# Retention's products as products of f16 halves, in a two-layer hybrid encoder trunk

## The chip, the core and the metric

One core of one Trainium2 chip runs the whole program. The metric is the device time of one execution in microseconds (us). All tables and lines below are from one profiled execution, unless they are said to be a median of runs. The engines are called PE (TensorE, the matrix engine; PEld is its loading of weights), DVE (VectorE), ACT (ScalarE), POOL (GpSimd) and SP (SyncE, which here only issues DMAs). L123 is line 123 of the kernel before, unless the kernel after is named.

## The reference

```python
D_MODEL, SEQ, DEPTH, CHUNK = 1024, 2048, 2, 64      # f32 throughout
...
def chunkwise_retention(q, k, v, cos, sin):
    q = apply_rotary(q, cos, sin)
    k = apply_rotary(k, cos, sin) * (dk ** -0.5)
    log_g = jnp.log1p(-jnp.exp2(-5.0 - jnp.arange(h)))
    intra_decay = jnp.exp(jnp.abs(idx[:, None] - idx[None, :])[None] * log_g[:, None, None])
    k_decay = jnp.exp((CHUNK - 1 - idx)[None, :] * log_g[:, None])
    q_decay = jnp.exp((idx + 1.0)[None, :] * log_g[:, None])
    chunk_decay = jnp.exp(CHUNK * log_g)
...
    att = jnp.einsum("bnihd,bnjhd->bnhij", qc, kc) * intra_decay[None, None]
    o_intra = jnp.einsum("bnhij,bnjhe->bnihe", att, vc)
    kv = jnp.einsum("bnjhd,hj,bnjhe->bnhde", kc, k_decay, vc)
    def step(state, kv_n):
        return state * chunk_decay[None, :, None, None] + kv_n, state
    _, states = lax.scan(step, zeros, moveaxis(kv, 1, 0))
    o_inter = jnp.einsum("bnihd,hi,bnhde->bnihe", qc, q_decay, states)
    return rms_norm(o_intra + o_inter)

def hybrid_layer(x, norm_gain, w_in, w_out, rel_bias, cos, sin):
    hn = rms_norm(x, norm_gain)
    proj = hn @ w_in                              # (2048, 1024) @ (1024, 4096)
    aq, ak, av, ag, rq, rk, rv, rg = jnp.split(proj, cuts, axis=-1)       # 512 columns each
    ya = chunked_rel_attention(aq, ak, av, rel_bias)       # 8 heads x 64, own chunk + 8 before
    yr = chunkwise_retention(rq, rk, rv, cos, sin)         # 4 heads x 128
    y = jnp.concatenate([ya * silu(ag), yr * silu(rg)], axis=-1)
    return x + y @ w_out
```

Two such layers follow one another, and the result is normalised once more. The change concerns retention (the four einsums above and the rotation in front of them) and the scale of the norm's gain.

## The kernel before

**Halves.** All dense products of the kernel are exact to about f32 although PE is fed with f16: each operand is split into a high half (the f16 rounding) and a low half (what is left, again in f16), and a product is three f16 products that add up in one PSUM bank: high times high, high times low, low times high. The splitting takes a copy on ACT (the high half) and a subtraction on DVE (the low half), in every place. So that nothing overflows or vanishes in f16, weights and rows are scaled by powers of two found from their sums of squares (`norm_scale`, L141); the inverse scales are undone later by column factors (`mul_cols`, L178, used in `T_units`, L341, and `V_units`, L397). Retention alone computes with f32 operands.

**Stages.** A startup (L1131 to L1228, an order written out by hand as a string of step names) loads x, normalises the first eight tiles of 128 tokens and prepares the first weights. Then each layer `l` runs four groups `s`. A group is two attention heads and one retention head. Each group runs four blocks `n` of 512 tokens. For a block, `dense_T` (L605) computes the four projections that are needed transposed, q, k, rq and rk (j = 0 to 3), each as 24 matmuls of 512 columns (L688), and `dense_V` (L695) computes the value and gate projections of the four tiles `a` of the block, 24 matmuls of 512 columns each (L708). These are cut into rounds: after every 8 matmuls the generator yields, so a block has 24 rounds. After the groups of a layer follows the output projection `wout` (L966), in the same rounds.

**What runs between the rounds.** `run` (L1043) does three things after each round: `tick`, which issues what `later(k, fn)` has put off by k rounds; one step of `attention` (L727) of the previous block, which itself steps `retention` (L802); and some steps of the background work in `bg` (conversion of the next weights `prep_T`, `prep_V`, `prep_O`, the rotary tables, the norms of later input tiles). The order of PE, ACT, DVE and POOL is the order in which the program issues: `manual_schedule` (L40) fixes it, and each of these engines executes in order. SP's queue is fixed by hand in the startup only; later the scheduler places its DMAs.

**Attention.** A block has 8 units (4 tiles by 2 heads), one per three rounds. A unit's scores go to one PSUM tile S, of which there is one buffer (L742, matmuls L749 and L750); DVE adds the bias and finds the maximum (L753), ACT takes the exponential (L756) and a high half (L758), POOL the low half (L759), a transposing DMA turns both (L761, tile pT), and one unit later PE multiplies with v (L769 to L771).

**Rotation.** ACT moves the projection of rq or rk out of PSUM into `rot` (L639, f32, 128x512), SP copies it with its halves exchanged to `swp` (L643, L644), three rounds later POOL multiplies both with the tables of cosines and sines and adds them (L647 to L649, the function `turn`).

**Retention.** Each tile of 128 tokens has two steps, in different rounds. In the first, PE computes the scores of keys and queries (L809) and turns the keys with a product by the identity (L812), ACT copies the turned keys with the key decay as a column factor (L814, ktok), and DVE multiplies the scores with the decay mask (L815, dT). In the second, PE adds dT times rv (L818) and the queries times the state (L820) in one place and ktok times rv, the tile's part of the state, in another (L822); DVE updates the state (L825); ACT squares the output for its norm (L831), DVE (L832) and POOL (L833) make the factor of the norm. Two rounds later DVE applies factor and gate (L837).

**Memory.** PSUM has three pools: psD, 2 banks for the dense products, psS for the scores, psR with 4 banks for retention, attention's output and small things. In SBUF, `w4` has four buffers of 128x1024 f32 for weights on their way in and tiles of x; `wh` and `wl` hold the converted weights; `hT` holds the normalised, transposed input of a layer, 128x8x512 per block and half.

**Scale of the gain.** `gain_scale` (L160) squares the norm's gain, sums it over the partitions by a product with ones (`allsum`, L319), and takes an inverse power of two from the exponent; it is called once in the startup, ahead of the first token's norm (`rms_of`, L195), and once in group 1 for layer 2, its two steps put off by 2 and 10 rounds (L1255 to L1257).

## Time and profile before

| | before |
|---|---|
| median of 3 runs | 2116.52 us (2115.85 to 2116.53) |
| profiled execution, whole time | 2114.12 us |
| its span, first to last instruction | 2112.3 us |
| mean clock that TensorE was granted | 0.994 of full |
| instructions | 37,845, of them 13,636 matmuls |
| DMA | 305 MB, 63% of 16 engines' time |

The retention lines on PE, by the trace: 128 products L809, 120 transposes L812, 128 products L818, 120 L820 and 120 L822 (an f32 product counts as two matmuls in the records). DMA issues that the change touches or that lie beside what it touches (the row of the page: tiles, queue, count, KB each, median us from issue to landing):

```profile
q<-qq SPq DMA_DIRECT2D x128, 128.0 KB, 2.6
swp<-rot SPq DMA_DIRECT2D x128, 128.0 KB, 2.4
```

To read the lines of a timeline: start in us from the span's start, length in us, engine, line, operation, output<-inputs by the names of tiles, shapes; in square brackets how long the engine had been idle and what released it. A matmul's shown length is modelled: what it costs PE is the distance from its start to the next one's. A line of the stretches gives, for a window of time, its length and then the busy time and the instructions of PE, PEld, DVE, ACT and POOL, the granted clock as a share, the DMA engines' busy share and the GB/s moved. For orientation: startup to about 50 us, the first group to about 230, then the groups of layer 1 to about 890, its output projection to about 1100, layer 2 after that.

### The profile page before, as it was taken

How to read it: one execution, taken by the hardware profiler on the slowest of the kernel's cores; microseconds unless marked ns; L12 is line 12 of the kernel's file. 1: busy time of each engine (PE TensorE's matmuls, PEld its weight loads, DVE VectorE, ACT ScalarE, POOL GpSimd, SP SyncE). 2: the span in 40 equal slices, each digit the busy share in tenths (PEclk: the TensorE clock that was granted, in tenths of full speed). 3: DMA queues.
4: the chain of work that ended last, by engine and by line, in shares of the span. 5: the costliest groups of instructions: out<-in, count | busy, mean ns of one | idle time of the engine just before them, and what ended most of it. 6: DMA issues, size and time to landing. Idle time of an engine off the chain costs nothing. (4 is left out here: it accounts for less than half of the span.)

```text
span 2112.3 us, 37845 instructions
## 1 busy us (share of the span) xinstructions
PE 2039.2 (97%) x13636; PEld 1109.4 (53%) x13636; DVE 1058.5 (50%) x3334; ACT 1024.9 (49%) x2034; POOL 695.7 (33%) x701
## 2 busy tenths in 40 slices
PE   7887999999999999989999999999999999999998
PEld 4444555555555555544444555555555555555543
DVE  7566555344534443456653435443544354336543
ACT  7445555446544544545443446444564454445432
POOL 1333343333433433321002433443344334333100
PEclk9999999999999999999999999999999999999999
DMA  8677664459545854789864546554685466548874
GB/s 250 144 152 155 155 148 112 99 111 209 121 103 110 156 145 96 153 168 261 224 167 105 118 95 140 112 119 94 146 186 118 96 147 149 117 93 180 196 207 120
DMA packets 611900, 305.15 MB, mean 144 GB/s; under 512 B 425440, under 2 KB 568288, under 8 KB 611712
## 3 DMA queue, kind: packets, MB, share of 16 engines
q1 hardware_dynamic: 611712, 302.73, 63.3%
q8 instruction: 107, 1.75, 0.4%
q14 instruction: 81, 0.66, 0.1%
HBM read 123.26 MB, written 41.98 MB: 78 GB/s over the span
## 5 line engine op out<-in xcount | busy, mean ns | idle before, releaser
L759 POOL TENSOR_TENSOR pq<-sc,pq 128x640 f16<-128x640 f32 (+4 forms) x256 | 319.5, 1248 | 837.1 <-ACT pq L758 374.9
L756 ACT ACTIVATE sc<-sc,mq,cT 128x640 f32<-128x640 f32 (+4 forms) x256 | 218.5, 854 | 609.8 <-DVE mq L755 363.0
L708 PE MATMUL dV<-whV,hTh 128*128 128x512 f16 x1024 | 389.1, 380 | 7.1 <-DVE gt L721 4.6
L708 PE MATMUL dV<-wlV,hTh 128*128 128x512 f16 x1024 | 389.1, 380 | 2.3 <-DVE wlV L333 2.3
L708 PE MATMUL dV<-whV,hTl 128*128 128x512 f16 x1024 | 389.1, 380 | 0.0
L688 PE MATMUL dT<-hTh,whT 128*128 128x512 f16 x1008 | 383.2, 380 | 4.4 <-DMA hTh<-rhn 4.4
L688 PE MATMUL dT<-hTl,whT 128*128 128x512 f16 x1008 | 383.0, 380 | 0.5 <-DMA hTl<-rln 0.5
L688 PE MATMUL dT<-hTh,wlT 128*128 128x512 f16 x1008 | 383.0, 380 | 0.0
L708 PEld LDWEIGHTS <-hTh 128*128 128x128 f16 x2048 | 200.2, 98 | 219.2 <-issue 10.3
L688 PEld LDWEIGHTS <-whT 128*128 128x128 f16 x2016 | 196.8, 98 | 214.9 <-issue 12.2
L753 DVE CUSTOM_DVE_ANT_0 sc<-S,bias 128x640 f32<-128x640 f32 (+4 forms) x256 | 189.3, 739 | 207.8 <-PE S L750 174.0
L996 PE MATMUL dO<-whO,yhy 128*128 128x512 f16 x512 | 194.5, 380 | 4.8 <-DVE hTh L999 1.9
L996 PE MATMUL dO<-whO,yly 128*128 128x512 f16 x512 | 194.8, 380 | 2.1 <-DMA yly<-rly 2.1
L996 PE MATMUL dO<-wlO,yhy 128*128 128x512 f16 x512 | 194.5, 380 | 0.1
L758 ACT ACTIVATE pq<-sc 128x640 f16<-128x640 f32 (+4 forms) x256 | 171.5, 670 | 8.1
L996 PEld LDWEIGHTS <-yhy 128*128 128x128 f16 x1024 | 100.2, 98 | 119.7 <-issue 7.1
L833 POOL TENSOR_TENSOR rss<-rss,mhalf 128x1 f32<-128x1 f32 x128 | 89.0, 695 | 210.7 <-DVE rss L832 191.7
L708 PEld LDWEIGHTS <-hTl 128*128 128x128 f16 x1024 | 100.4, 98 | 106.0 <-issue 5.2
L749 PE MATMUL S<-k,q 128*128 128x128 f16 (+3 forms) x592 | 142.3, 267 | 11.5 <-DVE mq L753 10.7
L688 PEld LDWEIGHTS <-wlT 128*128 128x128 f16 x1008 | 98.8, 98 | 97.6 <-issue 0.8
L719 DVE SCALAR_TENSOR_TENSOR v<-dV,v 128x128 f16<-128x128 f32 x128 | 37.2, 290 | 206.4 <-ACT rv L718 205.6
L769 PE MATMUL o<-v,pT 128*128 128x65 f16 x1120 | 129.3, 193 | 11.1 <-DMA pT<-pq 11.0
(309 smaller groups left out, 3326.5 us busy)
## 6 DMA issues: line engine op xcount, KB each, us to landing
q<-qq SPq DMA_DIRECT2D x128, 128.0 KB, 2.6
swp<-rot SPq DMA_DIRECT2D x128, 128.0 KB, 2.4
yyy<-y_d SPq DMA_DIRECT2D x32, 512.0 KB, 4.2
stT<-in_w_in_dram SPq DMA_DIRECT2D x28, 512.0 KB, 5.4
stV<-in_w_in_dram SPq DMA_DIRECT2D x26, 512.0 KB, 4.4
k<-kk SPq DMA_DIRECT2D x128, 64.0 KB, 2.0
tabc<-tab SPq DMA_DIRECT2D x32, 256.0 KB, 2.9
tabs<-tab SPq DMA_DIRECT2D x32, 256.0 KB, 3.0
```

The costliest lines, as they stand in the source:

```text
L688: pe.matmul(ps, w_[:, j, kt, :], h_[:, kt, :], start=(m == 0), stop=(m == 23))
L708: pe.matmul(ps, h_[:, kt, a * P:(a + 1) * P], w_[:, kt, :], start=(m == 0), stop=(m == 23))
L719: dve.scalar_tensor_tensor(out=st.v[:, a, :, 65:129], in0=pv_, scalar=2.0 ** -16, in1=vh_, op0=ALU.mult, op1=ALU.subtract)
L749: pe.matmul(o, st.q[:, hx, 0, cs], k_, start=True, stop=False)
L753: dve.tensor_tensor_reduce(out=v, in0=S[:, 0:w], in1=g.bias[hx][:, 640 - w:640], scale=1.0, scalar=-3.0e38, op0=ALU.add, op1=ALU.max, accu ...
L756: act.activation(v, v, AF.Exp, bias=m[:, 0:1], scale=g.c[:, 0:1])
L758: act.activation(pq[:, 0:w], v, AF.Copy)
L759: pool.tensor_tensor(pq[:, w:2 * w], v, pq[:, 0:w], op=ALU.subtract)
L769: pe.matmul(o[:, 0:65], u.p[:, b, :], v_[:, 0:65], start=(b == 0), stop=False)
L833: pool.tensor_tensor(ss, ss, mhalf, op=ALU.pow)
L996: pe.matmul(ps, h_[:, kt, :], w_[:, kt, :], start=(m == 0), stop=(m == 23))
```

## The change

Retention's four f32 products become three f16 products each, in the manner of the dense ones. What is new in detail:

- The rotated queries are kept as three planes of f16, high, low and high times 2^-11, the keys as two. The f32 values before the rotation lie in the space of the first two planes, the rotation's sum is left in `swp`, and a new function `halve` splits it, one round after `turn`: a copy on ACT, a subtraction on DVE, and for the queries one more copy on ACT.
- The keys are turned by one transposing DMA per block (`tokens`) in place of four products with the identity; both halves at once. The key decay, which was a column factor of that copy, moves to rv as a column factor (`V_units`), and its reciprocal into the mask (`T_units`), where rv is used with dT.
- rv is split where it leaves PSUM: high on ACT, low on DVE, and high times 2^-11 on ACT.
- dT and the state are split by a new function `apart`: a copy on ACT scaled by 2^-11, and the rest on DVE. The mask product goes to PSUM first. The state is now updated in place, and its decay is an ACT operation of its own.
- The column factors urq and urk are gone, rot leaves PSUM with a fixed factor, and the factors go into the norm's `re`, which gets clamps.
- `gain_scale` finds the scale in two steps: after the first the gain is scaled and raised to the fourth power, summed once more, and the scale is refined. It has one hop over PE and one yield more.
- Space: `w4` has three buffers instead of four; the fourth weight section of the startup is staged in the space of block 1's `hT`, the input tiles 8 to 11 are loaded into the space that tiles 4 to 7 had (`late[0:4]`), and the preparation of layer 2's value weights stages its sections 2 and 3 in `q` and converts them first.

```diff
@@ pools
-    w4 = ctx.enter_context(tc.tile_pool(name="w4", bufs=4))
+    w4 = ctx.enter_context(tc.tile_pool(name="w4", bufs=3))
@@ gain_scale
-        gk = gsb[:, l * KT:(l + 1) * KT]
-        dve.tensor_tensor_reduce(out=m, in0=gk, in1=gk, scale=1.0, scalar=0.0, op0=ALU.mult, op1=ALU.add, accum_out=ss)
-        ss = lowp(ss, f"g{l}")
+        raw = gsb[:, l * KT:(l + 1) * KT]
+        dve.tensor_tensor_reduce(out=m, in0=raw, in1=raw, scale=1.0, scalar=0.0, op0=ALU.mult, op1=ALU.add, accum_out=ss)
+        mb = lowp(ss, f"g{l}")
+        yield
+        s_, i_ = norm_scale(allsum(mb, f"g{l}", 2.0 ** -60), f"g{l}", None, -1)
+        g.i = b2.tile([P, 1], F32, tag="gi", name=f"gi{l}")
+        dve.tensor_copy(g.i, i_)
+        dve.tensor_scalar(gk, raw, s_[:, 0:1], None, op0=ALU.mult)
+        dve.tensor_tensor(gk, gk, gk, op=ALU.mult)
+        dve.tensor_tensor(gk, gk, gk, op=ALU.mult)
         dve.tensor_tensor_reduce(out=m, in0=gk, in1=gk, scale=1.0, scalar=0.0, op0=ALU.mult, op1=ALU.add, accum_out=ss)
+        mb = lowp(ss, f"h{l}")
         yield
-        s_, i_ = norm_scale(allsum(ss, f"g{l}", 2.0 ** -60), f"g{l}", None, -1)
+        m2 = allsum(mb, f"h{l}", 2.0 ** -60)
+        dve.tensor_scalar(e2, m2.bitcast(I32), 23, None, op0=ALU.logical_shift_right)
+        dve.tensor_scalar(e2, e2, 9.0, None, op0=ALU.add)
+        dve.tensor_scalar(e2, e2, 3, 23, op0=ALU.logical_shift_right, op1=ALU.logical_shift_left)
+        dve.tensor_scalar(i2, e2, float(111 << 23), None, op0=ALU.add)
...
-        dve.tensor_copy(g.i, i_)
+        dve.tensor_tensor(g.i, g.i, i2.bitcast(F32), op=ALU.mult)
@@ T_units
-        if j == 2:
-            g.urq = mul_cols("urq", iv[2], None, 2.0 ** -10, nm)
         if j == 3:
-            g.urk = mul_cols("urk", iv[3], None, 2.0 ** -10, nm)
+            g.qk = mul_cols("qk", iv[2], iv[3], 1.0, nm)
+            dve.tensor_scalar(g.msk, g.msk, g.rd, 2.0 ** (-7 - g.s), op0=ALU.mult, op1=ALU.mult)
@@ V_units
-        g.urv = mul_cols("urv", iv[1], None, 2.0 ** -10, nm)
+        g.urv = mul_cols("urv", dcs[:, s:s + 1], None, 2.0 ** -11, nm)
...
-        yield
-        dve.tensor_tensor(gk, gk, gk, op=ALU.mult)
-        dve.reciprocal(gk, gk)
+        g.re = mul_cols("re", iv[1], g.qk, 2.0 ** (31 + s), nm)
+        act.activation(g.re, g.re, AF.Copy, scale=gk[:, 0:1])
+        yield
+        for u in (gk, g.re):
+            dve.tensor_tensor(u, u, u, op=ALU.mult)
+            dve.reciprocal(u, u)
+        dve.tensor_scalar(g.re, g.re, EPS, 2.0 ** -120, op0=ALU.mult, op1=ALU.max)
+        dve.tensor_scalar(g.re, g.re, 2.0 ** 120, None, op0=ALU.min)
         g.ra = mul_cols("ra", gk, dcs[:, 8 + s:9 + s], 1.0, nm)
-        g.re = mul_cols("re", gk, None, EPS, nm)
@@ dense_T, evacuate
-                u = g.urq if j == 2 else g.urk
-                rot = b2.tile([P, 512], F32, tag=f"rot{j}", name=f"rot{nm}_{j}")
-                act.activation(rot, ps, AF.Copy, scale=u[:, 0:1])
+                w = 5 - j
+                rot = b2.tile([P, w, 512], F16, tag=f"rot{j}", name=f"rot{nm}_{j}")
+                raw = rot[:, 0:2].rearrange("p a c -> p (a c)").bitcast(F32)
+                act.activation(raw, ps, AF.Copy, scale=2.0 ** -16)
...
-                        pool.tensor_tensor(rot, rot, st.tabc, op=ALU.mult)
+                        pool.tensor_tensor(raw, raw, st.tabc, op=ALU.mult)
                         pool.tensor_tensor(swp, swp, st.tabs, op=ALU.mult)
-                        pool.tensor_tensor(rot, rot, swp, op=ALU.add)
-
-                    later(4 if j == 2 and first else 3, turn)
+                        pool.tensor_tensor(swp, raw, swp, op=ALU.add)
+
+                    def halve():
+                        act.activation(rot[:, 0], swp, AF.Copy)
+                        dve.tensor_tensor(rot[:, 1], swp, rot[:, 0], op=ALU.subtract)
+                        if j == 2:
+                            act.activation(rot[:, 2], rot[:, 0], AF.Copy, scale=2.0 ** -11)
+
+                    def tokens():
+                        st.kt = b1.tile([P, KT, P], F16, tag="ktok", name=f"kt{nm}")
+                        sp.dma_start_transpose(out=st.kt, in_=rot.rearrange("p a c -> p (a c)"))
+
+                    d = 4 if j == 2 and first else 3
+                    later(d, turn)
+                    later(d + 1, halve)
+                    if j == 3:
+                        later(5 if first else 11, tokens)
@@ dense_V
-            rv = gp.tile([P, P], F32, tag="rv", name=f"rv{nm}_{a}")
+            rv = gp.tile([P, 3, P], F16, tag="rv", name=f"rv{nm}_{a}")
...
-            act.activation(rv, ps[:, P:256], AF.Copy, scale=g.urv[:, 0:1])
+            act.activation(rv[:, 0], ps[:, P:256], AF.Copy, scale=g.urv[:, 0:1])
...
+            dve.scalar_tensor_tensor(out=rv[:, 1], in0=ps[:, P:256], scalar=g.urv[:, 0:1], in1=rv[:, 0],
+                                     op0=ALU.mult, op1=ALU.subtract)
...
+            act.activation(rv[:, 2], rv[:, 0], AF.Copy, scale=2.0 ** -11)
@@ retention
+    def products(out_, pairs):
+        for i, (w_, m_) in enumerate(pairs):
+            pe.matmul(out_, w_, m_, start=(i == 0), stop=(i + 1 == len(pairs)))
+
+    def apart(dst, src):
+        act.activation(dst[:, 0], src, AF.Copy, scale=2.0 ** -11)
+        dve.scalar_tensor_tensor(out=dst[:, 1], in0=dst[:, 0], scalar=-2.0 ** 11, in1=src, op0=ALU.mult, op1=ALU.add)
...
-            pe.matmul(r1[:, 0:P], st.rk[:, cs], st.rq[:, cs], start=True, stop=True)
-            dT = b1.tile([P, P], F32, tag="dT", name=f"dT{nm}")
-            if not last:
-                pe.transpose(r1[:, P:2 * P], st.rk[:, cs], ident)
-                kt_ = b1.tile([P, P], F32, tag="ktok", name=f"ktok{nm}")
-                act.activation(kt_, r1[:, P:2 * P], AF.Copy, scale=dcs[:, s:s + 1])
-            dve.tensor_tensor(dT, r1[:, 0:P], g.msk, op=ALU.mult)
+            products(r1[:, 0:P], [(st.rk[:, i, cs], st.rq[:, j, cs]) for i, j in ((0, 0), (0, 1), (1, 0))])
+            dT = b1.tile([P, 2, P], F16, tag="dT", name=f"dT{nm}")
+            dve.tensor_tensor(r1[:, P:2 * P], r1[:, 0:P], g.msk, op=ALU.mult)
+            apart(dT, r1[:, P:2 * P])
             yield
             r2 = psR.tile([P, 512], F32, tag="small", name=f"r2{nm}")
-            pe.matmul(r2[:, 0:P], dT, st.rv[a], start=True, stop=(t == 0))
+            rv = st.rv[a]
+            terms = [(dT[:, 0], rv[:, 0]), (dT[:, 0], rv[:, 1]), (dT[:, 1], rv[:, 2])]
             if t > 0:
-                pe.matmul(r2[:, 0:P], st.rq[:, cs], ring["state"], start=False, stop=True)
+                sh = ring["halves"]
+                terms += [(st.rq[:, 0, cs], sh[:, 0]), (st.rq[:, 1, cs], sh[:, 0]), (st.rq[:, 2, cs], sh[:, 1])]
+            products(r2[:, 0:P], terms)
             if not last:
-                pe.matmul(r2[:, P:2 * P], kt_, st.rv[a], start=True, stop=True)
-                ns = b2.tile([P, P], F32, tag="state", name=f"state{nm}")
+                kh, kl = st.kt[:, a, :], st.kt[:, 4 + a, :]
+                products(r2[:, P:2 * P], [(kh, rv[:, 0]), (kh, rv[:, 1]), (kl, rv[:, 0])])
                 if t > 0:
-                    dve.scalar_tensor_tensor(out=ns, in0=ring["state"], scalar=(1.0 - 2.0 ** (-5 - s)) ** P,
-                                             in1=r2[:, P:2 * P], op0=ALU.mult, op1=ALU.add)
+                    ns = ring["state"]
+                    dve.scalar_tensor_tensor(out=ns, in0=r2[:, P:2 * P], scalar=2.0 ** (-7 - s), in1=ns,
+                                             op0=ALU.mult, op1=ALU.add)
...
+                ring["halves"] = b1.tile([P, 2, P], F16, tag="sh", name=f"sh{nm}")
+                apart(ring["halves"], ns)
+                act.activation(ns, ns, AF.Copy, scale=(1.0 - 2.0 ** (-5 - s)) ** P)
@@ startup
-    W.load(3)
+    w3 = hT_of(0, 1)[0].rearrange("p k c -> p (k c)").bitcast(F32)[:, 0:D].rearrange("p (k c) -> p k c", c=P)
+    sp.dma_start(w3, w_in[0, :, TSEC[3] * 512:TSEC[3] * 512 + P].rearrange("(k p) c -> p k c", p=P))
+    W.sts.append([(w3, 0, KT)])
...
-    go_on(gs, gs)
+    go_on(gs, gs, gs)
...
-                    push(norms_from_input(range(4 * n + 4, 4 * n + 8)), 21)
+                    push(norms_from_input(range(4 * n + 4, 4 * n + 8), late[0:4] if n == 1 else None), 21)
...
+                        later(18, lambda gr=gr: next(gr))
```

49 lines of the change are left out of this document (26 added, 23 removed).

## The prediction, made before the changed kernel had run

> **What bounds the kernel now.** I read the busy shares first, then the stretches, then the spacing of matmuls, then one block instruction by instruction.
>
> ```profile
> PE 2039.2 (97%) x13636; PEld 1109.4 (53%) x13636; DVE 1058.5 (50%) x3334; ACT 1024.9 (49%) x2034; POOL 695.7 (33%) x701
> ```
>
> TensorE is busy nearly throughout, VectorE and ScalarE half the time. By stretches (columns: span, then PE, PEld, DVE, ACT, POOL busy, clock, DMA share, GB/s):
>
> ```profile
> 50.00:100.00 50.00, 43.45 (x203) 20.04 (x201) 30.00 (x63) 22.79 (x43) 17.96 (x19) 0.93 0.60 139
> 150.00:230.00 80.00, 67.17 (x489) 37.27 (x488) 50.34 (x144) 42.65 (x78) 28.23 (x25) 1.00 0.80 167
> 440.00:650.00 210.00, 208.14 (x1460) 115.94 (x1458) 99.47 (x364) 110.84 (x231) 83.22 (x80) 1.00 0.61 136
> ```
>
> A whole group (440 to 650) runs at PE's pace, 99% busy; the first group (50 to 230) does not, PE waits there 15% of the time. So a matmul saved is worth its time in the later groups, unless a wait takes its place.
>
> The timeline's starts, not the modelled lengths, price a matmul:
>
> ```profile
> 601.33 0.38 PE L818 MATMUL r<-rv,dT 128*128 128x128 f32 x2
> 601.55 0.39 PE L820 MATMUL r<-state,rot 128*128 128x128 f32 x2
> 601.77 0.39 PE L822 MATMUL r<-rv,ktok 128*128 128x128 f32 x2
> 601.99 0.38 PE L708 MATMUL dV<-whV,hTh 128*128 128x512 f16 x1
> ...
> 604.61 0.22 PE L749 MATMUL S<-k,q 128*128 128x128 f16 x1
> 604.67 0.22 PE L750 MATMUL S<-k,q 128*128 128x128 f16 x1
> 604.73 0.38 PE L708 MATMUL dV<-whV,hTl 128*128 128x512 f16 x1
> ...
> 606.45 0.38 PE L809 MATMUL r<-rot,rot 128*128 128x128 f32 x2
> 606.67 0.27 PE L812 MATMUL r<-ident,rot 128*128 128x128 f32 x1
> 606.78 0.38 PE L708 MATMUL dV<-wlV,hTh 128*128 128x512 f16 x1
> ```
>
> An f32 product takes 0.22 us from start to start, the f32 transpose 0.11, an f16 product of the same shape 0.06 (four of them from 597.65 to 597.87: 0.055 each).
>
> **The change, part by part.** *Products.* A tile now pays 4 x 0.22 + 0.11 = 0.99 us; after, 12 f16 products x 0.055 = 0.66. It saves 0.165 at the scores step and 0.16 at the output step. 112 middle tiles save 0.325 (36.4); 8 first tiles of a group 0.275 (2.2), having no state product; 8 last ones 0.165 (1.3), having neither transpose nor update. Sum: 39.9 us. Bound on the price: if f16 weight loads were not hidden, 98 ns each by their row, 1488 products would cost 146 us against 123 now; I take 0.055, because L749 and L750 load new weights for each of theirs.
>
> *Added work off PE.* Per tile ScalarE loses the ktok copy (0.35) and gains rv's third half, apart's copies of dT and of the state, and the decay: four of 0.27 to 0.35, net +0.75; VectorE gains three of 0.29, +0.87. Per block of four tiles the rotated queries and keys add three ScalarE passes of 128x512 (0.63 each, by L758 at 512) and two VectorE ones (0.68, by L281). That is +4.9 us on each engine per block of some 53 us, from half busy to 59%: hidden on average. Where it is not is a matter of order.
>
> *The new wait.* halve() is issued one round (8 dense matmuls) after turn(), behind the evacuation of rot for the keys on ScalarE. Its first pass needs POOL's third product. One block, in group 3:
>
> ```profile
> 601.53 0.69 ACT L639 ACTIVATE rot<-dT,urkT 128x512 f32<-128x512 f32 x1 [0.59 <-PE dT L688]
> 602.43 1.26 POOL L647 TENSOR_TENSOR rot<-rot,tabc 128x512 f32<-128x512 f32 x1
> 604.99 1.27 POOL L649 TENSOR_TENSOR rot<-rot,swp 128x512 f32<-128x512 f32 x1
> 605.04 0.82 DVE L753 CUSTOM_DVE_ANT_0 sc<-S,bias 128x640 f32<-128x640 f32 x1 [1.85 <-POOL swp L648]
> 606.22 0.92 ACT L756 ACTIVATE sc<-sc,mq,cT 128x640 f32<-128x640 f32 x1 [3.33 <-DVE mq L755]
> ...
> 610.70 0.27 PE L749 MATMUL S<-k,q 128*128 128x256 f16 x1
> ...
> 617.09 0.19 PE L769 MATMUL o<-v,pT 128*128 128x65 f16 x1
> ```
>
> ScalarE is free at 602.2 and would now sit until T = 606.26, when the turn ends; VectorE behind it, for the subtraction. Both run in program order, so softmax of the unit whose scores were ready at 605.0 is behind them. Counted from T: copy 0.06 to 0.69; subtraction from 0.73, then the state (T+1.6), its half (1.93), its rest (2.26), decay and square (2.73), rss (3.07), and only there the sc pass, whose end (T+4.0) frees the one scores bank. Then by the distances of the rows above: exp at T+4.25, pq to 5.95, POOL to 7.4 (608.0 to 609.4 before), the transposing DMA's landing, 3.4 later, T+10.85. PE wants the bank at 610.70, T+4.44, less the 0.33 it saved on the way, T+4.1: just free. It wants pT at 617.09, T+10.83, less 0.49: T+10.35, so it waits 0.5.
>
> The same distances in the other blocks of a group: the fourth has 4.43 and 10.85, wait 0.5, and about 0.5 more a unit later, as prep_V's conversions (1.14 and 1.3) share the engines; the second has 4 to 5.4 and 10.1 to 11.6 with narrower tiles, wait 0.2; the first, where the next group's weights have just been converted, 2.68 and 9.08: the bank is late by 4.0 - 2.35 = 1.65 and pT by 0.65 more, with 0.5 to 1 for V_units' extra column operations and the keys' halve, say 3. A group of four blocks waits 0.5 + 0.2 + 1.0 + 3.0 = 4.7 and saves 16 x 0.325 = 5.2: a net 0.5. Seven groups give back 33 of their 36, but layer 2's first block, which has no attention beside it, waits nothing (its 3 stay): net gain 6. If halve's wait were covered instead, the gain would be 36; if each of the 21 later blocks of three waited a microsecond longer, a loss of 15.
>
> *First group.* There VectorE and ScalarE set the pace, so what they are given counts: the turn of the first block ends at 61.92, ScalarE's next row pass copy is at 61.59, so halve puts two passes (1.3) and a subtraction ahead of tokens 6 and 7, whose transposes PE awaits until 73.98: +2. Blocks 2 and 3 have VectorE back to back at 99 to 125 and 160 to 200: +2 to 3 each; the fourth +0.5; less about 1 of saved products. Sum +6.5 (bounds 2, if the waits of PE there hide it, to 15, if all 19 us of added VectorE work showed, less what products save).
>
> *gain_scale in two steps.* Twelve more VectorE operations of about 0.19 and a matmul hop of 0.25 between L316 and L196: 2.6 us; VectorE had 1.6 idle there before L98, waiting for positions. So the first token's product (L254, 8.89) comes some 1.1 later. The second call, for layer 2, and mask scale, clamps and reciprocals (a few of 0.2 to 0.3 per group) lie in VectorE's idle half.
>
> *DMA.* 32 more transposing DMAs of 128x1024, 3.4 to 4.0 us by rhn's rows, one per block, issued 5 rounds (11 us) ahead of use, at 61% DMA share: nothing, or their 1.3 of issue time (32 x 1.3 = 42 spread over SP) ahead of the next q loads, which have a round and more to spare. w4's third buffer less, W3 in hT's space and x tiles 8 to 11 loaded once tiles 4 to 7 are done (from 51 us, needed at 87): nothing; if a load came late, 5 once. The output stage: attention's tail of four tiles, +-1.
>
> Sum: -6 + 6.5 + 1.1 + 1 (tails) = +2.6. The profiled execution took 2114.1 (span 2112.3), the shown runs' median is 2116.5; so **2119**, no change that this kernel's measurement can tell (about 0.2%, 4 us).
>
> **Rivals.** *Halve's wait is covered* (faster): ScalarE's copies or POOL's turn come a microsecond earlier against PE than I count, since bank and pT miss by 0.5 in most blocks. Then the groups keep 30 of 36: 2116.5 - 30 + 7.6, about 2090 to 2096. For it: 49% idle, and blocks two to four are within 0.5 of even. Against: the first block misses by 2.3.
>
> *Waits bunch and PE's clock falls* (slower): in the first block of a group two waits of 1.65 and 0.65, and more behind, stand within 7 us. The trace has the pattern: waits of 1.3 (102.68) and 2.46 (107.86), each short of the 4 us ones, and then matmuls spaced 0.427 instead of 0.216, for 5 in a row; after 4.8 at 69.19, 13 of them. [...] At 13 x 0.211 = 2.7 and the deeper wait that leads to it (1 us more per block with wide attention, 21 of them): 7 x 2.7 = 19, to 2138; with half of the deeper waits 2148. The Trainium skill, "TensorE: Matmul & The Clock Gate", section "HAM oscillation" and the second failure mode behind it, holds that idling too short to be one long gap can also make the clock swing between half and full; the spacings of 0.427 above agree.
>
> *The products do not get cheaper*: weight loads show at 98 ns; 2116.5 + 22 and the rest, 2150. Against it stand L749 and L750.
>
> **How the numbers follow.** Forecast 0.45 (own range 2108 to 2130), covered 0.30, bunched 0.20, dear products 0.05. Faster by over 0.2%: 0.30 + 0.07 of the forecast = 0.37; within: 0.20; slower: 0.18 + 0.25 = 0.43. The range 2086 to 2143 takes in the covered case and most of the bunched one.
>
> **What would show it.** Retention's product lines should fall from 123 us of PE starts to 83. ScalarE's halve lines (two per queries, one per keys) should show 64 waits on POOL's last product of turn, 150 to 250 us in all, and PE new waits in stretches that had none (440 to 650): S on VectorE and o on the transposing DMA, 3 to 6 us a group, most in its first block. If those stretches keep 99% PE and shrink by 5 us a group, the walk from T is wrong and the time is near 2092. If the clock's share falls under 0.99 after 230 us, it is the bunched case. If L254's counterpart starts later than 10.5, the two steps cost more than counted.

## The result, and the profile after

Before ran in 2116.22 us (2115.85 to 2116.53, 4 runs), the changed kernel in 2270.90 us (2267.47 to 2272.83, 4 runs): ratio 1.0729, 95% interval 1.0711 to 1.0748. It became 155 us slower; 2119 had been forecast. The profiled execution after has a span of 2270.1 us against 2112.3, and a granted clock of 0.971 against 0.994. From here on lines are those of the kernel after: the dense products are L721 (was L688) and L741 (L708), attention's scores L785 (L749), its softmax L789 to L795 (L753 to L759), its products with v L805 to L807 (L769 to L771), halve L671 to L674, apart L844 and L845, retention's products L840. Lines of another run are numbered by that run's own kernel, so the same number can be another line.

The busy shares of the page after:

```profile
PE 2062.7 (91%) x14014; PEld 1066.1 (47%) x14014; DVE 1193.0 (53%) x3839; ACT 1171.5 (52%) x2522; POOL 697.8 (31%) x701
```

ScalarE and VectorE got 147 and 135 us more work in 158 us more span: by their shares neither is fuller than before by more than three points. PE's share fell from 97% to 91%. The stretches of the first and the third block of the third group in layer 1 (s = 2) show where (columns: stretch, length, then PE, PEld, DVE, ACT, POOL busy with counts, clock, DMA share, GB/s). Before:

```profile
470.40:524.30 53.90, 53.50 (x393) 29.97 (x392) 27.93 (x98) 34.69 (x73) 20.16 (x21) 1.00 0.91 200
575.40:628.70 53.30, 53.30 (x388) 30.18 (x388) 22.19 (x75) 22.00 (x46) 21.36 (x19) 1.00 0.48 103
```

After:

```profile
515.60:584.50 68.90, 57.68 (x404) 29.91 (x403) 33.73 (x119) 42.78 (x95) 21.49 (x23) 0.93 0.80 176
642.10:697.20 55.10, 52.56 (x403) 28.20 (x401) 27.25 (x99) 28.53 (x64) 21.63 (x19) 1.00 0.53 105
```

The third block, which has no background work, grew by 1.8 us. The first, which shares ScalarE and VectorE with the conversion of the next weights and, in this group, with the squares of the output weights, grew by 15, and its clock fell to 0.93. The same over the whole run, from the first dense matmul of each block to that of the next (the last block of a layer stands with its output stage; the first group ends at 259.8 us, where the second one's first product starts, later than the 230 given for orientation):

| us | before | after | halve and apart left out |
|---|---|---|---|
| startup and first group | 259.8 | 286.5 | 263.1 |
| first blocks of the seven other groups | 364.3 | 434.7 | 368.0 |
| second blocks, 7 | 348.5 | 383.2 | 338.6 |
| third blocks, 7 | 373.1 | 373.3 | 363.9 |
| fourth blocks, 5 | 267.7 | 268.5 | 261.1 |
| output stages of layers 1 and 2 | 254.8, 244.1 | 265.4, 258.6 | 252.4, 243.3 |
| span | 2112.3 | 2270.1 | 2090.3 |

The loss can be split by PE's distances from start to start. What goes beyond the spacing of an undisturbed row of the same shape is a wait, and a matmul of 512 columns that stands about 0.427 from the next instead of 0.216 ran at half speed. Waits grew from about 73 to 240 us, and matmuls at half speed from 31 to 177, which is 6.5 to 35.8 us. With 38 us of saved products: 167 + 29 - 38 = 158, the whole difference of the spans. Two of PE's groups before and after (idle time before the group, then what ended it):

```profile
L769 PE MATMUL o<-v,pT 128*128 128x65 f16 x1120 | 129.3, 193 | 11.1 <-DMA pT<-pq 11.0
L323 PE MATMUL msT<-mbT,ones 128*128 128x1 bf16 x28 | 4.7, 167 | 3.5 <-DVE mbT L316 3.4
L805 PE MATMUL o<-v,pT 128*128 128x65 f16 x1120 | 134.3, 197 | 50.8 <-DMA pT<-pq 47.2 <-DVE m2T L340 2.1 <-DVE ya L817 1.4
L338 PE MATMUL msT<-mbT,ones 128*128 128x1 bf16 x28 | 4.6, 165 | 30.8 <-DVE mbT L331 30.8
```

The first of each pair waits for attention's transposed probabilities (pT), the second for the sum of squares of a weight tile (msT). Both operands come out of chains of operations that run over ScalarE and VectorE.

What a wait looks like, in a third block (timeline after):

```profile
672.52 1.27 POOL L668 TENSOR_TENSOR swp<-rot,swp 128x512 f32<-128x512 f32 x1
673.82 0.63 ACT L671 ACTIVATE rot<-swp 128x512 f16<-128x512 f32 x1 [4.90 <-POOL swp L668]
674.49 0.69 DVE L672 TENSOR_TENSOR rot<-swp,rot 128x512 f16<-128x512 f32 x1 [7.94 <-ACT rot L671]
675.10 0.28 DVE L871 SCALAR_TENSOR_TENSOR state<-r,state 128x128 f32<-128x128 f32 x1
675.41 0.31 ACT L844 ACTIVATE sh<-state 128x128 f16<-128x128 f32 x1 [0.30 <-DVE state L871]
675.75 0.29 DVE L845 SCALAR_TENSOR_TENSOR sh<-sh,state 128x128 f16<-128x128 f16 x1 [0.38 <-ACT sh L844]
676.90 0.81 DVE L789 CUSTOM_DVE_ANT_0 sc<-S,bias 128x640 f32<-128x640 f32 x1
677.77 0.27 PE L785 MATMUL S<-k,q 128*128 128x256 f16 x1 [0.44 <-DVE mq L789]
679.77 1.39 POOL L795 TENSOR_TENSOR pq<-sc,pq 128x640 f16<-128x640 f32 x1 [2.08 <-ACT pq L794]
```

ScalarE stands 4.9 us before halve's copy, VectorE 7.9 behind it; then come the steps of the state, each on the other engine, and only then softmax. The scores product (L785) starts when the softmax pass L789 has freed the one scores bank.

In the second block of the same group, where conversions of weights stand between, the same start ends worse:

```profile
613.44 0.63 ACT L671 ACTIVATE rot<-swp 128x512 f16<-128x512 f32 x1 [3.22 <-POOL swp L668]
616.51 1.27 DVE L348 SCALAR_TENSOR_TENSOR wlT<-stT,sT,whT 128x1024 f16<-128x1024 f32 x1
617.70 0.55 DVE L789 CUSTOM_DVE_ANT_0 sc<-S,bias 128x384 f32<-128x384 f32 x1
...
622.27 0.29 DVE L856 TENSOR_TENSOR r<-r,msk 128x128 f32<-128x128 f32 x1
622.59 0.28 ACT L844 ACTIVATE dT<-r 128x128 f16<-128x128 f32 x1 [2.13 <-DVE r L856]
622.77 1.05 ACT L324 ACTIVATE whT<-stT 128x1024 f16<-128x1024 f32 x1
623.94 0.16 DVE L331 CAST mbT<-m1T 128x1 bf16<-128x1 f32 x1 [0.75 <-ACT whT L324]
624.15 0.16 PE L338 MATMUL msT<-mbT,ones 128*128 128x1 bf16 x1 [3.62 <-DVE mbT L331]
```

The last line is a PE wait of 3.6 us for a sum of squares whose turn had been put three rounds after its operands: the square on ScalarE (L324) stands behind dT's copy (L844), that behind the mask's product on VectorE (L856), that behind softmax and a conversion (L348), these behind halve. There the order of ScalarE and VectorE trails PE by more than the rounds of distance that the program leaves. VectorE's own idle time in that run says the same for halve's subtraction and for the rest of dT, each of which stands behind a copy on ScalarE:

```profile
L672 DVE TENSOR_TENSOR rot<-swp,rot 128x512 f16<-128x512 f32 x64 | 55.5, 868 | 267.1 <-ACT rot L671 266.9
L845 DVE SCALAR_TENSOR_TENSOR dT<-dT,r 128x128 f16<-128x128 f16 x128 | 36.9, 288 | 87.7 <-ACT dT L844 87.7
```

### The profile page after: what moved, and what is told of

The parts are those of the page before. It is cut to its first block, busy times and chain, and to the rows that moved or that the text cites. A ratio compares the mean times of both kernels' runs of the same rounds, so it can differ in the third digit from the quotient of the medians.

```text
span 2270.1 us, 39370 instructions
## 1 busy us (share of the span) xinstructions
PE 2062.7 (91%) x14014; PEld 1066.1 (47%) x14014; DVE 1193.0 (53%) x3839; ACT 1171.5 (52%) x2522; POOL 697.8 (31%) x701
## 5 line engine op out<-in xcount | busy, mean ns | idle before, releaser
L795 POOL TENSOR_TENSOR pq<-sc,pq 128x640 f16<-128x640 f32 (+4 forms) x256 | 319.4, 1247 | 787.2 <-ACT pq L794 386.9
L741 PE MATMUL dV<-whV,hTh 128*128 128x512 f16 x1024 | 397.2, 388 | 28.8 <-DVE gt L756 26.7
L741 PE MATMUL dV<-wlV,hTh 128*128 128x512 f16 x1024 | 397.2, 388 | 2.7 <-DVE wlV L348 2.7
L741 PE MATMUL dV<-whV,hTl 128*128 128x512 f16 x1024 | 395.8, 386 | 0.0
L721 PE MATMUL dT<-hTh,whT 128*128 128x512 f16 x1008 | 387.2, 384 | 7.8 <-DVE rot L672 3.4
L721 PE MATMUL dT<-hTl,whT 128*128 128x512 f16 x1008 | 386.7, 384 | 2.8 <-DMA hTl<-rln 2.8
L721 PE MATMUL dT<-hTh,wlT 128*128 128x512 f16 x1008 | 386.7, 384 | 0.0
L741 PEld LDWEIGHTS <-hTh 128*128 128x128 f16 x2048 | 200.0, 99 | 274.4 <-issue 42.8
L721 PEld LDWEIGHTS <-whT 128*128 128x128 f16 x2016 | 196.1, 99 | 234.7 <-issue 27.2
L882 POOL TENSOR_TENSOR rss<-rss,mhalf 128x1 f32<-128x1 f32 x128 | 93.8, 732 | 425.0 <-DVE rss L881 384.3
L789 DVE CUSTOM_DVE_ANT_0 sc<-S,bias 128x640 f32<-128x640 f32 (+4 forms) x256 | 188.3, 736 | 66.3 <-PE S L786 56.3
L672 DVE TENSOR_TENSOR rot<-swp,rot 128x512 f16<-128x512 f32 x64 | 55.5, 868 | 267.1 <-ACT rot L671 266.9
L805 PE MATMUL o<-v,pT 128*128 128x65 f16 x1120 | 134.3, 197 | 50.8 <-DMA pT<-pq 47.2
L785 PE MATMUL S<-k,q 128*128 128x128 f16 (+3 forms) x592 | 146.8, 274 | 31.2 <-DVE mq L789 25.6
L805 PEld LDWEIGHTS <-pT 128*128 128x128 f16 x1120 | 107.5, 99 | 100.4 <-DMA pT<-pq 70.4
L741 PEld LDWEIGHTS <-hTl 128*128 128x128 f16 x1024 | 101.8, 99 | 110.4 <-issue 12.9
```

Of the source, the lines that this page charges most:

```text
L672: dve.tensor_tensor(rot[:, 1], swp, rot[:, 0], op=ALU.subtract)
L721: pe.matmul(ps, w_[:, j, kt, :], h_[:, kt, :], start=(m == 0), stop=(m == 23))
L741: pe.matmul(ps, h_[:, kt, a * P:(a + 1) * P], w_[:, kt, :], start=(m == 0), stop=(m == 23))
L785: pe.matmul(o, st.q[:, hx, 0, cs], k_, start=True, stop=False)
L789: dve.tensor_tensor_reduce(out=v, in0=S[:, 0:w], in1=g.bias[hx][:, 640 - w:640], scale=1.0, scalar=-3.0e38, op0=ALU.add, op1=ALU.max, accu ...
L795: pool.tensor_tensor(pq[:, w:2 * w], v, pq[:, 0:w], op=ALU.subtract)
```

## The experiments

Every ratio is against the kernel before on the same chip. Differences between versions are differences of medians, some from different chips; on these the kernel before lay between 2114.5 and 2116.5. Edits are shown in part, and "..." marks what is left out. Theory H lays the loss on halve's wait, theory C on apart's chain; theory W says that late operands in an ordered queue are the cost, theory L that the added work is.

**Retention left as it was.** All the rest of the change was put into the kernel before (two of its hunks):

```diff
-    w4 = ctx.enter_context(tc.tile_pool(name="w4", bufs=4))
+    w4 = ctx.enter_context(tc.tile_pool(name="w4", bufs=3))
...
-    go_on(gs, gs)
+    go_on(gs, gs, gs)
```

> The kernel before with only the parts of the change that are not retention: the gain's scale in two steps, w4 with three buffers, the fourth weight section and the tiles 8 to 11 staged elsewhere, layer 2's value weights staged in q. Retention stays f32. Theory of the prediction: 2117 to 2123 (1.1 us for the gain's scale, at most 5 for a late load). Theory S (the loss sits in staging and loads, as PE's new waits for sums of squares msT suggest, 33 us of them): 2150 or more, with those waits present.

Measured 2114.0 us, ratio 0.9995 (0.9983 to 1.0006): nothing that can be told from no change, and no dearer than the 2117 to 2123 expected. PE waits 3.4 us for msT, as before the change. Staging, buffers and the gain's scale are not where the time went.

**Halve left out, apart left out, both left out.**

```diff
-                        pool.tensor_tensor(swp, raw, swp, op=ALU.add)
+                        pool.tensor_tensor(rot[:, 0], raw, swp, op=ALU.add)
...
-                    later(d + 1, halve)
```
```diff
-            dve.tensor_tensor(r1[:, P:2 * P], r1[:, 0:P], g.msk, op=ALU.mult)
-            apart(dT, r1[:, P:2 * P])
+            dve.scalar_tensor_tensor(out=dT[:, 0], in0=r1[:, 0:P], scalar=2.0 ** -11, in1=g.msk, op0=ALU.mult, op1=ALU.mult)
```

In these three runs as many f16 products are computed as in the kernel after, with the high plane in the place of the low one. Without halve, the turning DMA of the keys moves one plane instead of two. Without apart, the state's decay and the mask product's pass through PSUM go as well.

> The kernel after, but POOL's last product of the rotation writes an f16 plane itself and halve is left out: neither the low halves of rotated queries and keys nor the third plane are made, the high plane stands in for them in the same number of products, and the turning DMA moves the high plane only. After measured 2271; PE's products alone would give about 2080. Theory H (ScalarE's wait for POOL in halve, 155 us of idle, and VectorE's behind it is most of the loss): 2160 or less. Theory C (the chain VectorE, ScalarE, VectorE of apart, which ties the two engines to each other four times per tile, is most of it): 2220 or more. If the two only hurt together, both this and the run without apart fall by more than half of the loss.

> The kernel after, but dT and the state are kept as one f16 plane, written by VectorE in one operation each as in the kernel before: apart's copies and rests, the decay and the mask's pass through PSUM are left out (the state isn't decayed), and the high plane stands in for the rest in the same number of products. Theory C: 2180 or less. Theory H: 2230 or more, with ScalarE's waits before halve unchanged at 150 us.

> The kernel after without halve and without apart, as in the two runs before it. What is left of the change are 12 f16 products for 4 f32 ones and a transpose, rv's halves, the turning DMA and the rest. Theories H and C alike: 2075 to 2100 (2116 less 38 of saved products, plus a few us of waits in the first group). If it stays above 2120, a third cause (rv's halves at each evacuation, the staging, or the turning DMA) holds the difference.

Measured 2148.5 (ratio 1.0155, 1.0125 to 1.0184), 2166.2 (1.0238, 1.0209 to 1.0268) and 2088.4 (0.9871, 0.9827 to 0.9915), two runs each. Leaving halve out takes 122 us away, apart 105, both 182: more than half each, less than the sum together. Neither H nor C alone is it. What is left without them is some 28 us faster than before, so most of the 38 us of saved products arrives, as the same two blocks show in that run:

```profile
470.40:524.50 54.10, 52.76 (x407) 28.14 (x404) 27.42 (x103) 35.78 (x76) 20.35 (x21) 1.00 0.90 205
574.40:626.40 52.00, 52.00 (x402) 28.24 (x399) 23.39 (x80) 22.35 (x48) 21.43 (x20) 1.00 0.50 108
```

In the third block PE is busy throughout, and it takes 52.0 us against 53.3.

**The same work in another order.** Here the whole computation is kept, each operation on its engine, and only issued later. Halve's copies come two rounds after the turn instead of one and its subtraction a round behind them (the exchange of the keys' halves moves a round later with them); apart's steps, and the state's decay behind them, come a round apart:

```diff
-                    later(d + 1, halve)
+                    later(d + 2, halve)
+                    later(d + 3, rest)
...
-        act.activation(dst[:, 0], src, AF.Copy, scale=2.0 ** -11)
-        dve.scalar_tensor_tensor(out=dst[:, 1], in0=dst[:, 0], scalar=-2.0 ** 11, in1=src, op0=ALU.mult, op1=ALU.add)
+        later(1, lambda: act.activation(dst[:, 0], src, AF.Copy, scale=2.0 ** -11))
+        later(2, lambda: dve.scalar_tensor_tensor(out=dst[:, 1], in0=dst[:, 0], scalar=-2.0 ** 11, in1=src,
+                                                  op0=ALU.mult, op1=ALU.add))
```

> The kernel after, whole computation, with halve issued later and in two steps: ScalarE's copies two rounds after the turn instead of one, VectorE's rest a round behind them; the keys' exchange one round later. Every operation is still there. Leaving halve out gave 2149. Theory W (the engines stand behind a late operand; the work itself fits): about 2150 to 2165, ScalarE's idle before the copy under 20 us of 155. Theory L (the added work, some 105 us on ScalarE and VectorE in halve, is the price): 2230 or more.

> The kernel after, whole computation, with apart spread over rounds: ScalarE's copy one round after VectorE's product, VectorE's rest one after that, the state's decay one after that. halve as in the kernel after. Leaving apart out gave 2166. Theory W: 2165 to 2190. Theory L: 2240 or more.

> Both rearrangements, whole computation, the same operations on the same engines as the kernel after. Leaving both out gave 2088. Theory W: 2090 to 2110, so faster than the kernel before. Theory L: 2180 or more. In between: the waits are worth the difference to 2271 and the work the difference to 2088.

Measured 2186.5 (halve moved), 2204.0 (apart spread) and 2138.5 (both; ratio 1.0106, 1.0089 to 1.0123). Moving alone, with no operation less, gives 84 of the 122 us that halve costs, 67 of apart's 105, and 132 of the 182 of both. Order is some 70% of what the two cost. The expectations of theory W were all too low, by 14 to 28 us, so it isn't all.

One part of theory W failed here. ScalarE was to stand under 20 us before halve's copy once it came later, and it stood 93.8 with halve moved and 161.4 with both moved, against 155.5 in the kernel after. What fell was VectorE's wait behind that copy, from 267.1 to 44.2 and 58.7 (here with both moved):

```profile
L671 DVE TENSOR_TENSOR rot<-swp,rot 128x512 f16<-128x512 f32 x64 | 45.8, 716 | 58.7 <-ACT rot L674 58.4
```

So ScalarE's wait for POOL, taken by itself, can stay as long as it was while 132 us come back. That VectorE's wait is what made it dear fits these numbers, but no run moved the subtraction alone.

**The chain without a change of engine.**

```diff
-        act.activation(dst[:, 0], src, AF.Copy, scale=2.0 ** -11)
+        dve.tensor_scalar(dst[:, 0], src, 2.0 ** -11, None, op0=ALU.mult)
```

> The kernel after, whole computation, with apart's first copy moved from ScalarE to VectorE, so that dT's chain has no change of engine; VectorE gets 248 operations of about 0.3 more (74 us), ScalarE as much less. halve as in the kernel after. Theory W in its form 'the changes of engine in order are the cost': 2190 to 2230. Theory L with VectorE as the bound: slower than 2271.

Measured 2233.9 (ratio 1.0559, 1.0538 to 1.0580). VectorE has 248 operations and 63 us of work more and the kernel is 37 us faster than the kernel after, so theory L with VectorE as the bound doesn't hold here. Whether the gain comes from fewer changes of engine or from the 62 us that ScalarE lost, this run can't tell. It is a third of what leaving apart out gives, just beyond the dear end of what theory W had named.

**Later still, and work taken off ScalarE.** In the run with both moved, halve's copy still waited for POOL; in the next one, one round later, it did not (group of the copy in the two runs):

```profile
L674 ACT ACTIVATE rot<-swp 128x512 f16<-128x512 f32 x64 | 40.2, 628 | 161.4 <-POOL swp L668 161.4
```
```profile
L674 ACT ACTIVATE rot<-swp 128x512 f16<-128x512 f32 x64 | 39.3, 615 | 9.5 <-POOL swp L668 9.5
```
```diff
-                    later(d + 2, halve)
+                    later(d + 3, halve)
```

> The run with both rearrangements (2138.5), with halve one more round later: copies three rounds after the turn, the rest four, the keys' exchange four rounds after their evacuation. There ScalarE still sat 161 us before halve's copy, as POOL begins the turn only behind a subtraction of softmax. Theory W: these waits are what is left; with under 60 us of them the time is 2100 to 2120. Theory L (what is left is the work beside the weights' preparation, 1100 to 1170 us on each engine): 2130 to 2140, though the waits go.

Measured 2132.2 (ratio 1.0075, 1.0060 to 1.0090). 152 us of ScalarE's idle went, and the kernel gained 6; theory W had named 2100 to 2120, and the answer is theory L's, 2130 to 2140 though the waits go. By then nearly all these waits were no price. Idle time, even with a releaser's name on it, isn't one. (In this run, too, the subtraction and the exchange come a round later.)

The same kernel with the state's decay and the third planes of queries and rv on POOL (the planes a round later; one of three hunks):

```diff
-                            act.activation(rot[:, 2], rot[:, 0], AF.Copy, scale=2.0 ** -11)
+                            later(1, lambda: pool.tensor_scalar(rot[:, 2], rot[:, 0], 2.0 ** -11, None, op0=ALU.mult))
```

> The run before it with three of the change's ScalarE operations on POOL, whole computation: the state's decay, the queries' third plane and rv's third plane, a round or more after their operands are ready; ScalarE loses 120 x 0.31 + 32 x 0.63 + 128 x 0.31 = 97 us. Theory L: 20 us or more faster than the run before it. Theory W: within 8 us of it. If POOL's work delays softmax's subtraction or holds up VectorE, slower than it.

Measured 2139.9 (1.0109, 1.0092 to 1.0126), 8 us slower than the run before it, though ScalarE's busy time fell from 1153 to 1074. POOL needs 0.652 and 1.494 us for the two shapes below, for which ScalarE took 0.31 and 0.63:

```profile
L760 POOL TENSOR_SCALAR rv<-rv 128x128 f16<-128x128 f16 x128 | 83.5, 652 | 21.3 <-ACT rv L754 18.8
L676 POOL TENSOR_SCALAR rot<-rot 128x512 f16<-128x512 f16 x32 | 47.8, 1494 | 2.4 <-ACT rot L674 0.7
```

PE's waits at L808 for pT, which POOL's subtraction of softmax feeds, grew from 5.4 to 15.5 us (the run before, then this one):

```profile
L808 PE MATMUL o<-v,pT 128*128 128x65 f16 x1120 | 132.0, 195 | 5.4 <-DMA pT<-pq 4.1 <-DVE yr L890 1.1
L808 PE MATMUL o<-v,pT 128*128 128x65 f16 x1120 | 132.7, 195 | 15.5 <-DMA pT<-pq 15.5
```

These 10 us are about what the run lost. So 79 us less on ScalarE showed no gain here, but as POOL got 187 more, ScalarE's fullness isn't ruled out cleanly.

**Where the rest is.** Against the run without halve and apart, the run with halve three rounds late was 7.5 and 4.8 us longer in the two blocks with the squares of the output weights and some 11.5 in each output stage. So those squares were moved to the third block, which has no other background work, once with that run and once with the kernel before. With that run a second thing was changed: in the last block of each layer halve comes two rounds after the turn, not three.

```diff
-                if n == 0 and s == 2:
+                if n == 2 and s == 2:
                     push(prep_Omax(l, go), 13)
```

```diff
-                    later(d + 3, halve)
-                    later(d + 4, rest)
+                    e = 2 if (s, n) == (NSW - 1, NS - 1) else 3
+                    later(d + e, halve)
+                    later(d + e + 1, rest)
```

> The run with halve three rounds after the turn (2132), with the squares of the output weights (prep_Omax, eight passes of 1.05 us on ScalarE) moved from the first block of group 2 to its third, which has no other background work, and halve two rounds after the turn in the last block of a layer. Against the run that left halve and apart out, the run before it was 8 us longer in each of the two blocks with prep_Omax and some 12 in each stage around the output projection; elsewhere they agree. If the remainder is background work that meets the change's work in the same block: 2105 to 2120. If it is something else in these blocks: 2125 or more.

> The kernel before with prep_Omax moved to the third block of group 2, nothing else, so that the run above has a fair neighbour. Before waited 0.7 and 1.6 us in the two blocks from 470 on in layer 1 and 0.5 and 1.4 in layer 2: 2112 to 2116.

Measured 2123.0 (ratio 1.0040, 1.0026 to 1.0053; 2116.9 to 2127.2 in 8 runs) and 2110.2 (0.9981, 0.9972 to 0.9990). The first lies between the two answers (2105 to 2120, or 2125 and more), the second just under its 2112 to 2116. With that run, the first blocks fell from 381.0 to 361.8 and the third ones rose from 364.1 to 371.5. The move in the kernel before is the only version here with the whole computation that is faster than before beyond the noise, by 0.2%. Ahead of the second output stage the rearranged kernel is level with before (its last third block starts at 1812 against 1815); what it gained in the groups it loses in the two output stages (263.2 and 256.7 against 254.8 and 244.1). The earlier halve in the last block did nothing for these: they were 264.0 and 254.7 without it. In each of the five runs that move the keys' exchange two rounds (this one, the two before it with halve three rounds late, and two of the three below), PE waits 10.5 to 14.3 us there for yly, the low half of the output projection's operand, which a transposing DMA brings. It is 2.1 in the kernel before and 3.3 with halve two rounds late. Why this transfer comes late stays open.

**Late halve or spread apart.** Each alone, the other left out, by the edits shown above (late means three rounds after the turn, as before the squares were moved):

> The kernel after with apart left out (dT and state as one f16 plane, as in the earlier run without apart) and halve three rounds after the turn. Without both it was 2088, with both in their late form 2132. If late halve holds the rest: 2115 or more; if the two add: about 2110; if only their meeting costs: under 2100.

> The kernel after with halve left out (high planes written by POOL, as in the earlier run without halve) and apart spread over three rounds. If spread apart holds the rest: 2115 or more; if the two add: about 2110; if only their meeting costs: under 2100.

Measured 2131.4 (1.0065, 1.0042 to 1.0088) and 2119.1 (1.0012, 0.9999 to 1.0024). Against 2088 late halve costs 43, spread apart 31, both 44. Each run gives its own first answer, that it holds the rest, which leaves nothing for the other: beside late halve, spread apart is free. They meet in the same stretches. The first blocks take 380.0 us with late halve alone, 382.4 with spread apart alone and 381.0 with both, against 368.0 with neither. The output stages are 19, 8 and 23 us longer than with neither, the first group only 0.2, 2.2 and 0.7. PE's waits change their name: with late halve alone it stands 22.9 us before pT and 4.4 before dT's products, with both 4.1 and 30.5.

**dT's split in one go on VectorE**, in the run with the squares moved:

```diff
-            apart(dT, r1[:, P:2 * P])
+            dve.tensor_scalar(dT[:, 0], r1[:, P:2 * P], 2.0 ** -11, None, op0=ALU.mult)
+            dve.scalar_tensor_tensor(out=dT[:, 1], in0=dT[:, 0], scalar=-2.0 ** 11, in1=r1[:, P:2 * P], op0=ALU.mult,
+                                     op1=ALU.add)
```

> The run with prep_Omax moved (2123), with dT's split in one go on VectorE behind the mask's product, without ScalarE; the state's split stays spread. Spread apart's price shows as PE's waits before dT's products (34 us in the run with halve three rounds late). If the three rounds of the spread are that price: those waits fall under 15 us and the time is 2100 to 2115. If VectorE's or ScalarE's fullness in these blocks is, the waits move to other tiles and the time stays at 2118 to 2128.

Measured 2135.2 (1.0094, 1.0080 to 1.0108), 12 us slower and outside both answers, though the waits moved as the second had it. PE's waits before dT's products did go, and those before pT came in their place. The run with the spread, then this one:

```profile
L844 PE MATMUL r<-rv,dT 128*128 128x128 f16 x384 | 45.6, 220 | 27.3 <-DVE dT L849 16.1 <-ACT dT L848 11.1
L809 PE MATMUL o<-v,pT 128*128 128x65 f16 x1120 | 131.4, 195 | 2.5 <-DMA pT<-pq 1.3 <-DVE rl L815 1.0
```
```profile
L844 PE MATMUL r<-rv,dT 128*128 128x128 f16 x384 | 43.4, 219 | 3.4 <-DVE dT L862 2.6 <-ACT rhy L924 0.4
L809 PE MATMUL o<-v,pT 128*128 128x65 f16 x1120 | 130.8, 194 | 26.5 <-DMA pT<-pq 25.3 <-DVE ya L821 1.0
```

So the last 35 to 44 us over 2088 show at whichever operand comes last in the full stretches, and PE's waits for yly alone are some 10 us longer than in the run with neither. What makes these stretches full stays open. VectorE's busy time alone doesn't order the runs: it is 1122 us with late halve alone (2131) and 1157 with spread apart alone (2119). A run that takes work off VectorE alone was not made.

## Why the prediction was wrong

By the terms of its sum: the seven later groups, forecast at -6, came out at +106 (70 in the first blocks, 35 in the second, 1 in third and fourth ones); the first group, forecast at 6.5 and 1.1 for the gain's scale, at 27; the output stages, forecast at 1, at 25. The mechanism that it named was there, and the step that failed is the one from one block to the others.

- *Products*: right. L840's 1488 products took 113.0 us from start to start, 28.1 of it waits between them: 85, against 83 forecast. The third block without halve and apart is 1.3 us shorter than before, the 4 x 0.325 of the sum.
- *Halve's wait*: there, and of the size named. ScalarE stood 155.5 us before 47 of the 64 copies (64 waits and 150 to 250 forecast). But its size said little of its price: with both moved it was 161.4, and 132 us had come back.
- *The walk from T*: right where it was made. In the third block shown above T is 673.79; the sc pass ends at T + 3.9 (4.0 forecast), softmax's subtraction at T + 7.4 (7.4), the bank is late by 0.6 (forecast: just free). The third and fourth blocks came out at before's time (373.3 against 373.1, 268.5 against 267.7): their waits, about 1.3 us each, take what the products save. The block that was walked (575 to 629 in the kernel before) is a third one, the kind without background work.
- *The other blocks*: this is the step that failed. The second block's wait of 0.2 was about 9, 8, 3, 6, 8 and 6 us by PE's distances (none in the last group of layer 2). The first block's "say 3" was about 11, 14, 7, 4, 8, 16 and 9, the fourth of these in the block of layer 2 that was to wait nothing. The walk treated a block as one wait, with everything in place again a few microseconds later. It took the conversions as half a microsecond here or there, where each holds the same two engines for 1.05 to 1.3 us.
- *Added work off PE*: "hidden on average", priced at nothing, is the other half of that step. The sum was right: 4.9 us per engine and block are 157 in all, and the engines got 147 and 135. But apart put VectorE, ScalarE, VectorE in a row into each of a tile's two steps, and left out, it is worth 105 us (67 by order alone). The walk had the state's steps in it, as part of halve's tail only, and dT's not at all.
- *First group*: 6.5 forecast, 26.7 with the startup. Without apart and halve it is 3.3. *Output stages*: 1 forecast, 10.6 and 14.5 measured; without apart and halve they are 2.4 and 0.8 shorter than before. The forecast gave attention's tail there "+-1" without a walk.
- *gain_scale*: the first token's product starts at 9.8, 0.9 later than before (1.1 forecast). *DMA*: kt lands in 3.2 us; with the staging nothing showed, as said.
- *Rivals*: "covered" is what the rearranged runs came near to in the steady blocks (52.0 us at 100% PE), and nowhere else. "Bunched waits" had the right sign and the right blocks, but its 2138 to 2148 is far short: half-speed matmuls cost 29 us more, where it names 19, and the waits themselves 167. Its step from a microsecond more of waiting to half speed is shown by no run (see the last section). "Dear products" did not happen: at 85 us for 1488 products, 0.057 each, the weight loads stayed hidden.

## What to carry to other kernels

In engines that run in order, the cost of a new operation is not its share of busy time: ask what it waits for and what stands behind it, above all where it makes two engines take turns, and in the block where background work is densest, not in the typical one. Issue each step of a split a round after the step that feeds it; that alone gave back 132 of the 182 us here. A saving of 38 us on a busy TensorE pays only if the work that it brings to the other engines makes none of its operands late.

## What the runs showed of the hardware

Half speed follows neither from the length of one wait nor from a sum of waits alone. In the kernel after, 4.00 us lay between two of PE's starts from 620.15 on, and no matmul of the next 8 us was slow; after 1.75 us from 561.35 on and 2.07 from 563.76 on, the next eight dense ones were. In the kernel before, 1.30 and 2.46 us (from 102.68 and 107.86 on) were followed by slow matmuls, and 1.65 and 2.10 (from 163.99 and 168.57 on), the same sum in a shorter stretch, were not. The Trainium skill, "TensorE: Matmul & The Clock Gate", section "HAM oscillation", speaks of gaps over about 3.4 us; here shorter ones among others did it, as its second failure mode allows.

POOL and VectorE hold each other up. In the run with halve three rounds late:

```profile
889.72 1.26 POOL L667 TENSOR_TENSOR swp<-swp,tabs 128x512 f32<-128x512 f32 x1
890.88 1.28 DVE L246 SCALAR_TENSOR_TENSOR rly<-yyy,sy,rhy 128x1024 f16<-128x1024 f32 x1 [3.21 <-DMA pT<-pq]
891.06 2.23 POOL L668 TENSOR_TENSOR swp<-rot,swp 128x512 f32<-128x512 f32 x1
892.28 1.02 DVE L815 TENSOR_TENSOR rl<-rl,kaV 128x1 f32<-128x1 f32 x1
```

L815 takes 0.16 us alone; here it ends with POOL's product L668. That product takes 1.27 alone and 2.23 here, where L246 still ran for the first 1.1 of them. The Trainium skill, "SBUF — State Buffer", section "SBUF: two separate sides", has this as an exclusive lock on the port pair that the two engines share. It is no part of the difference between before and after in total: what VectorE's operations take beyond the median of their row adds up to about 35 us before and 38 after. Single waits hold some of it: in the second block shown above, L812 took 1.22 us beside POOL's L666, just ahead of the mask's product. In the run with halve three rounds late the sum is 54 and with the squares moved 61, so it may be a part of what stays open there.
